# Norm and gate sums later, other PSUM banks, a chunk of products ahead of waits, and a compressed softmax spread over four slots: a three-layer transformer kernel on one core

## The chip, the cores and the metric

The kernel runs on one core of one Trainium2 chip. Its time is the device time of one execution in microseconds (us); lower is better. Engines are named as in the profile: PE is TensorE's matmul, PEld its weight load, DVE is VectorE, ACT is ScalarE, POOL is GpSimd, SP is SyncE (it issues most DMAs). PSUM is the memory into which PE writes.

## The reference, cut to what matters

512 positions, width 1024, float32. Three layers follow one another: a "forgetting" attention, a dilated attention, each with a gated addition behind it, and a block with a convolution branch, a sparse-attention branch with three parts (compressed, selected, window) and a feed-forward network.

```python
h = h + fox_mixer(rms_norm(h, fox_norm), fox_w_in, fox_b_f, fox_w_out)     # 16 heads of 64
h = h + (p[0] @ ple_w_up[0]) * sigmoid(h @ ple_w_gate[0])
h = h + dilated_mixer(rms_norm(h, dil_norm), dil_w_in, dil_w_out)          # 8 heads of 128, 3 patterns
h = h + (p[1] @ ple_w_up[1]) * sigmoid(h @ ple_w_gate[1])
x = rms_norm(h, final_norm)

def fox_mixer(h, w_in, b_f, w_out):
    q, k, v, z, f_logit = split(h @ w_in)
    c = cumsum(log_sigmoid(f_logit + b_f))                 # one gate per head and position
    s = q @ k.T / 8 + c[:, None] - c[None, :]              # causal
    return (softmax(s) @ v * silu(z)) @ w_out

def dilated_mixer(h, w_in, w_out):
    # q, k, v for 3 patterns (window 128 stride 1, 512 stride 4, 2048 stride 16), z once;
    # each pattern's softmax is weighted by its share of the common denominator
    return (o * silu(z)) @ w_out

def second_block(x, ...):
    hn = rmsnorm(x, norm1_g)
    a_b, a_c, a_x, q, kc, vc, ksl, vsl, kwn, vwn, g_nsa, g_merge = split(hn @ w_in)
    y_a = a_b * causal_dwconv(a_c * a_x, conv_a_w)
    q, k_sel, k_win = rope(rmsnorm(...))
    k_cmp, v_cmp = rmsnorm(compress(kc)), compress(vc)     # 31 compressed positions
    p_c = masked_softmax(q @ k_cmp.T / 8)                  # the compressed part
    y_b = g0 * p_c @ v_cmp + g1 * selected + g2 * window   # 8 heads of 64, 2 groups of keys
    x = x + (sigmoid(g_merge) gating of y_a @ w_a_out and y_b @ w_b_out) @ w_o
    hn = rmsnorm(x, norm2_g)
    g, u = split(hn @ w_ffn_in)
    return x + (silu(causal_dwconv(g) + b) * u) @ w_ffn_out
```

## The kernel before, in words

**Products.** Activations lie transposed, as eight tiles of 128 features by 512 positions. Each float32 operand is kept as two parts, a high half (`a0h`, `whi`) in the format that PE takes at full rate and the remainder (`a0l`, `wlo`), and `mm3` (L142) makes three products of each pair: high times high, high times low, low times high. These are the products of 128x512 on L144 to L146 (and L248 to L250 where positions are the rows).

**Weights.** `Weights` streams one 128x1024 unit at a time in a fixed plan: SP loads it (`wraw`), ACT copies the high half (`whi`, L74), DVE subtracts (`wlo`, L85). `pump` starts the next ones whenever a chunk of products is issued; the position of these instructions among the others of ACT, DVE and SP is therefore set by the order in which chunks are called. Every engine takes its own instructions in the order in which the program issues them.

**Chunks.** `t_unit` gives the products of one unit as two chunks of 12, and its evacuation behind the second. `k_outer` gives nine: `ko[0]` to `ko[7]` each make the nine products of one input tile with three units at once, into three accumulators, and `ko[8]` evacuates them. `n_chunk` gives eight chunks (two per unit) into four accumulators, with one evacuation after another in the last two. `narrow` gives two (placing the low halves, and 16 products). `run` calls a list, `weave` spreads attention slots evenly among chunks.

**PSUM.** `bank(tag)` hands out eight banks in turn: three `acc`, two `s`, two `t`, one `o`. Who asks for a bank waits until its former contents have been read.

**Norms.** A row's sum of squares is gathered by ACT (squares, L290) and POOL (`nacc`, L291), eight times. `norm_sums` (L295 to L303) then lets PE sum it over the partitions by products with one column; `norm_factors` makes the reciprocal root by a chain of small DVE operations (L310, L267 to L270); `norm_rows` spreads it over all partitions by PE and ACT (`rb`). Since products are made with unnormed data, `rb` is wanted only at the evacuation. In the fox mixer these are `fin1` and `fin2`, among the chunks on L581; `gate_sums` there starts the gate's chain (DVE L519 to L525), whose result `c` goes to DRAM and comes back spread over all partitions as `cb` (`load_c`), for the first softmax.

**Slots.** An attention step j is a slot: finish a softmax that is open (reciprocal and scaling, L637 and L640 or L642), transpose the probabilities of step j - LAG by PE into a `t` bank, copied by ACT (`pt` L695, `dpt` L836), then make the scores of step j in an `s` bank, which DVE reads first (L624, or L824 and L825), and ACT's exponential (L628). Every sixth or fourth slot adds a product with the values (`pv_step`, bank `o`), gated by `zh` and fed to the output products as `a0h`, `a0l` and so on (`feed`, L327 and L328). In the dilated mixer head h's slots are woven among `dz` (its gate, evacuated as `zh` L611, ACT's tanh L615, `zs` L616), `dq` and `dk` of head h + 1; the last slots (eight in the fox mixer, six in the dilated) are woven among the first chunks of the output projection by `mixer_out` (L591), which then closes the pool, opens the next stage's (`ple_open`, eight loads of the residual `hA`) and runs the rest.

**Second block.** L1300 runs the query units `nq` (the bank list is `n_chunk`'s default, `acc`, `acc`, `acc`, `s`) with `fin1` after its fourth chunk; ahead of it the gated addition's last unit is read out of its `acc` by ACT (`th`, L750). L1313 runs the first chunks of the convolution branch (`conv`), with small steps among them: `tr_k` transposes the keys `kd` (ACT, L1049) into a `t` or an `s` bank and splits them (`k00h`, `k00l` L1070), `tr_q` the queries into a `t` bank, `cmp_k3` the compressed keys `kcn`, copied by ACT as `kc` (L1125). The slots after that (L1279) hold, beside selected and window attention, the compressed part: `c_scores` in slots 1 and 19, `c_soft` (the softmax on [128, 16 x 32], DVE and one exponential) in slots 3 and 21, and `ct_step(p)`, its transposes, with step 2, 14, 26 and 38 of the transposes. `conv[5:]` and the merge gates are woven among them; `ev_ab` (L1173) multiplies an accumulator with `rb` and the convolution and feeds it (`b1h`).

Of the kernel before, what the change touches and what calls it, by code (L numbers as in the profile page):

```python
# [16 lines left out]
P = 128  # L17
# [110 lines left out]
class Net:  # L128
# [308 lines left out]
    def fox(self):  # L437
# [143 lines left out]
        run(ko[:7] + [fin1, ko[7], ch[0], ff[0], fin2, ko[8], ch[1], ff[1]] + ch[2:4])  # L581
        run([gate_sums] + ch[4:6] + [lambda: load_c(0), lambda: load_c(1)] + ch[6:])
# [8 lines left out]
    def mixer_out(self, tag, pair, es, res_src, i, slots):  # L591

        ko = self.k_outer([tag] * 3, [lambda a, n=n: self.ev_res(a, n) for n in range(3)], pair)
        weave(ko[:5], slots)
        es.close()
        self.ple_open(res_src, i)
        run(ko[5:])
        for n in range(3, 8):
            run(self.t_unit(tag, pair, self.full(), lambda a, n=n: self.ev_res(a, n), tag_ps="s" if n == 3 else "acc"))
# [167 lines left out]
    def dil(self):  # L767
# [122 lines left out]
        for h in range(8):  # L890
            if h % 4 == 0:
                vs = []
                for g in range(3):
                    vs += self.n_chunk("dv", residues if g else blocks, B, ev_v(g))
                weave(vs[:5], todo)
                run(vs[5:])
                todo = slots(h)
            ch = T("dz", ev_z(h))
            if h < 7:
                for g in range(3):  # L900
                    ch += T("dq", ev_q(h + 1, g)) + T("dk", ev_k(h + 1, g))
            n = 4 if h < 7 else 2
            weave(ch, todo[:n])
            todo = todo[n:]
# [42 lines left out]
    def block2(self):  # L947
# [174 lines left out]
        def cmp_k3():  # L1122
            p = self.bank("t")
            nc.tensor.transpose(p[:, :64], kcn.rearrange("p a d -> p (a d)"), self.ident[:64, :64])
            nc.scalar.activation(kc, p[:, :64], AF.Copy)  # L1125
# [114 lines left out]
        def c_soft(g):  # L1240
            sp, x = self.bank("o"), pcs[g]
            for qb in range(4):
                nc.tensor.transpose(sp[:, qb * P : (qb + 1) * P], x[:, qb * P : (qb + 1) * P], self.ident)
            pcs[g] = x = x.rearrange("p (q h k) -> p q h k", q=4, h=4)
            st = aa.tile([P, 2, 4, 4], F32, name="cst", tag="cst", bufs=1)
            bc = lambda y: y[:, :, :, None].broadcast_to([P, 4, 4, 32])
            m = mcmp[:, :P].rearrange("p (q k) -> p q k", q=4)[:, :, None, :].broadcast_to([P, 4, 4, 32])
            v.tensor_tensor(x, sp.rearrange("p (q h k) -> p q h k", q=4, h=4), m, ALU.add)
            v.tensor_reduce(st[:, 0], x, mybir.AxisListType.X, ALU.min)
            v.tensor_tensor(x, x, bc(st[:, 0]), ALU.subtract)  # L1250
            nc.scalar.activation(x, x, AF.Exp, scale=-1.0)
            v.tensor_reduce(st[:, 0], x, mybir.AxisListType.X, ALU.add)
            v.reciprocal(st[:, 1], st[:, 0])
            v.tensor_tensor(st[:, 1], st[:, 1], gc[:, :, 4 * g : 4 * g + 4], ALU.mult)
            v.tensor_tensor(x, x, bc(st[:, 1]), ALU.mult)
# [23 lines left out]
        def slot(j):  # L1279
            self.soft_end()  # L1280
            u = j - LAG
            if 0 <= u < 48:
                self.t_step(aa, pts, probs, u)
                if u % 12 == 2:
                    ct_step(u // 12)
            if j < 48:
# [3 lines left out]
                if j in (3, 21):  # L1290
                    c_soft(j // 21)
# [7 lines left out]
        ch = self.n_chunk("nq", lhs, A, ev_nq)  # L1299
# [11 lines left out]
        for i in range(4):  # L1311
            conv += T("ac", ev_ac(i)) + T("ax", ev_ax(i)) + T("ab", ev_ab(i))
        run([conv[0], gate_sums, conv[1], L(tr_k, 0, 0), L(tr_k, 0, 1), L(rope_k, 1), conv[2], cmp_k3, L(tr_q, 3), conv[3],  # L1313
             L(tr_k, 1, 0), tr_g, conv[4], L(tr_k, 1, 1)])
# [263 lines left out]
```

## Time and profile before

| | before |
|---|---|
| median of 3 runs | 1738.43 us (1738.42 to 1739.5) |
| profiled execution | 1738.31 us |
| its span | 1736.5 us |
| PE busy | 1718.7 us, 99% of the span |
| DVE, ACT, POOL busy | 967.3, 672.8, 111.0 us |
| share of the chain of waits on PE | 92% |
| DMA share of 16 engines | 30.0% (172.36 MB) |

The span is the time between the first and the last instruction of the profiled execution, 1.8 us less than its device time. A row of a timeline gives the start, the length, the engine, the line, the operation and its tiles, and in brackets the idle time before it with what ended that. Records of pipelined products overlap: a 128x512 product is shown as 0.39 us long, while one starts every 0.23 us.

### The profile page before, as it was taken

The numbers are of one execution on the slowest core, as the hardware profiler recorded it, in microseconds if no ns is written. First come the engines' busy times: TensorE is split into PE (matmuls) and PEld (weight loads), VectorE is DVE, ScalarE is ACT, GpSimd is POOL, SyncE is SP. The second block draws the span as 40 slices with busy tenths as digits, with TensorE's granted clock in tenths as the row PEclk, the third lists the DMA queues.
The fourth block names the chain that finished last, engine by engine and source line by source line (L and its number), as shares of the span: only waits on it lengthen the run. The fifth ranks groups of instructions, "written<-read, shape, count | busy, mean of one in ns | idle before, by whom it ended". The sixth has DMA issues, their size and how long they took to land.

```text
span 1736.5 us, 21611 instructions
## 1 busy us (share of the span) xinstructions
PE 1718.7 (99%) x8512; PEld 1401.6 (81%) x8512; DVE 967.3 (56%) x1692; ACT 672.8 (39%) x1146; POOL 111.0 (6%) x88
## 2 busy tenths in 40 slices
PE   8999999999999999999999999999999999999999
PEld 6777777888978889978878786777788888888887
DVE  6477774543354543354555677776554675566332
ACT  5466663522222222222245444555522433333220
POOL 2000000100000000000000411000000222111000
PEclk9999999999999999999999999999999999999999
DMA  5422224323221223222233422112243533223431
GB/s 166 141 93 86 91 74 139 122 93 130 90 85 61 85 73 97 85 85 73 74 111 120 156 99 73 49 61 86 73 141 120 165 108 101 96 97 98 145 97 61
DMA packets 57350, 173.74 MB, mean 100 GB/s; under 512 B 7441, under 2 KB 7953, under 8 KB 57249
## 3 DMA queue, kind: packets, MB, share of 16 engines
q1 hardware_dynamic: 57248, 172.36, 30.0%
q8 instruction: 67, 1.10, 0.3%
q14 instruction: 35, 0.28, 0.1%
HBM read 161.82 MB, written 10.52 MB: 99 GB/s over the span
## 4 chain that ended last, share of the span: by engine, by line
PE 92%; DVE 4%; ACT 2%; POOL 1%; issue 0%; DMA 0%; SPq 0%; ACTq 0%; DVEq 0%
PE acc L144 21%; PE acc L146 20%; PE acc L145 20%; PE acc L248 3%; PE acc L250 3%; PE acc L249 3%; PE o L700 2%; PE t L692 2%; PE s L144 1%; PE s L145 1%; PE s L146 1%; DVE wlo L85 1%; PE s L248 1%; PE s L679 1%; PE s L250 1%; PE s L249 1%
## 5 line engine op out<-in xcount | busy, mean ns | idle before, releaser
L85 DVE TENSOR_TENSOR wlo<-wraw,whi 128x1024 fp32r<-128x1024 f32 x267 | 347.8, 1309 | 137.9 <-ACT whi L74 137.8
L74 ACT ACTIVATE whi<-wraw 128x1024 fp32r<-128x1024 f32 x267 | 279.2, 1050 | 158.7 <-PE acc L145 68.2
L628 ACT ACTIVATE pr<-pr,st 128x512 f32<-128x512 f32 (+3 forms) x160 | 93.6, 586 | 155.3 <-DVE st L825 83.3
L291 POOL TENSOR_TENSOR nacc<-nacc,sq 128x512 f32<-128x512 f32 x35 | 47.9, 1376 | 1186.9 <-ACT sq L290 1186.4
L781 DVE TENSOR_TENSOR dqk<-acc,nacc 128x512 f32<-128x512 f32 x24 | 26.1, 1099 | 61.6 <-PE s L814 57.5
L695 ACT ACTIVATE pt<-t 128x512 f32<-128x512 f32 (+3 forms) x128 | 51.0, 424 | 19.7 <-PE t L692 19.3
L1413 ACT ACTIVATE fy<-fcv,fcw 128x512 f32<-128x512 f32 x22 | 18.0, 816 | 100.0 <-DVE fcv L1408 100.0
L1426 POOL TENSOR_TENSOR act<-fs,fu 128x512 f32<-128x512 f32 x22 | 43.3, 1969 | 191.0 <-DVE fu L1425 174.0
L692 PE MATMUL t<-ident,pr 128*128 128x128 f32 x320 | 51.1, 274 | 2.3 <-ACT pt L695 1.2
L692 PEld LDWEIGHTS t<-ident,pr 128*128 128x128 f32 x320 | 39.9, 140 | 14.5 <-DVE pr L640 1.6
L144 PE MATMUL acc<-a0h,whi 128*128 128x512 f32 x112 | 47.9, 427 | 1.2 <-DVE zh L611 1.2
L824 DVE SCALAR_TENSOR_TENSOR pr<-dist,s 128x128 f32<-128x128 f32 (+1 forms) x96 | 24.9, 315 | 42.2 <-PE s L818 42.2
L637 DVE RECIPROCAL st<-st 128x1 f32<-128x1 f32 x160 | 24.1, 158 | 40.4 <-ACT pr L628 40.4
L144 PE MATMUL acc<-b4h,whi 128*128 128x512 f32 x113 | 45.7, 404 | 0.0
L144 PE MATMUL acc<-b7h,whi 128*128 128x512 f32 x113 | 44.6, 395 | 0.0
L146 PE MATMUL acc<-b7h,wlo 128*128 128x512 f32 x113 | 44.6, 395 | 0.0
L145 PE MATMUL acc<-b7l,whi 128*128 128x512 f32 x113 | 44.4, 393 | 0.0
L146 PE MATMUL acc<-a0h,wlo 128*128 128x512 f32 x112 | 44.3, 395 | 0.0
L144 PE MATMUL acc<-b5h,whi 128*128 128x512 f32 x113 | 44.2, 391 | 0.0
L145 PE MATMUL acc<-a0l,whi 128*128 128x512 f32 x112 | 44.1, 394 | 0.0
L145 PE MATMUL acc<-a1l,whi 128*128 128x512 f32 x112 | 43.9, 392 | 0.2 <-DVE a1l L331 0.2
L145 PE MATMUL acc<-b4l,whi 128*128 128x512 f32 x113 | 44.1, 390 | 0.0
(1107 smaller groups left out, 4686.5 us busy)
## 6 DMA issues: line engine op xcount, KB each, us to landing
wraw<-in_dil_q SPq DMA_DIRECT2D x24, 512.0 KB, 3.3
wraw<-in_dil_k SPq DMA_DIRECT2D x24, 512.0 KB, 3.3
wraw<-in_dil_v SPq DMA_DIRECT2D x24, 512.0 KB, 3.3
wraw<-in_f_g SPq DMA_DIRECT2D x22, 512.0 KB, 3.5
wraw<-in_f_u SPq DMA_DIRECT2D x22, 512.0 KB, 3.5
wraw<-in_f_o SPq DMA_DIRECT2D x22, 512.0 KB, 3.4
wraw<-in_gate SPq DMA_DIRECT2D x16, 512.0 KB, 3.3
wraw<-in_b_gm SPq DMA_DIRECT2D x16, 512.0 KB, 3.5
```

What stands on the lines that cost most here:

```text
L74: nc.scalar.activation(hi, t, AF.Copy)
L85: self.nc.vector.tensor_tensor(lo, t, hi.bitcast(F32), ALU.subtract)
L144: mm(acc, wh, xh, start=start, stop=False)
L145: mm(acc, wh, xl, start=False, stop=False)
L146: mm(acc, wl, xh, start=False, stop=stop)
L248: self.nc.tensor.matmul(a, sh, mh, start=(k == 0), stop=False)
L249: self.nc.tensor.matmul(a, sh, ml, start=False, stop=False)
L250: self.nc.tensor.matmul(a, sl, mh, start=False, stop=(k == KT - 1))
L291: nc.gpsimd.tensor_tensor(self.nacc[i], self.nacc[i], sq, ALU.add)
L628: self.nc.scalar.activation(pr, pr, AF.Exp, scale=-1.0, bias=st[:, 0:1], accum_out=st[:, 1:2])
L692: nc.tensor.transpose(tp[:, c : c + P], pr[:, c0 + kb * P : c0 + (kb + 1) * P], self.ident)
L695: nc.scalar.activation(pts[h][:, self.KOFF[kb] : self.KOFF[kb] + b - a], tp[:, a:b], AF.Copy)
```

## The change

Six places are rewritten. In the fox mixer `fin1`, `fin2` and `gate_sums` are called later among the chunks. In `mixer_out`, used by both mixers, six chunks are woven among the last slots, and one fewer is left for after the pool is closed. In the dilated mixer's last head both chunks of `dz` are called ahead of its two slots, not one ahead of each. The `nq` chunk takes its accumulators in the order `s`, `t`, `acc`, `acc`. In the second block `conv[2]` is called ahead of `tr_k`, the later chunks move up, and `cmp_k3` takes an `s` bank. `c_soft` is cut into four steps, in four slots from 3 and 21 on, and the first `ct_step` goes with step 5 of the transposes. No computation is added or left out.

```diff
@@ -578,8 +578,8 @@
         lhs = lambda x, b: x[:, b * P : (b + 1) * P]
         ch = self.n_chunk("v", lhs, A, ev_v(0), ("s", "s", "t", "t"))
         ff = self.narrow("f", A, ev_f, "acc")
-        run(ko[:7] + [fin1, ko[7], ch[0], ff[0], fin2, ko[8], ch[1], ff[1]] + ch[2:4])
-        run([gate_sums] + ch[4:6] + [lambda: load_c(0), lambda: load_c(1)] + ch[6:])
+        run(ko[:8] + [ch[0], fin1, ch[1], ff[0], ch[2], fin2, ko[8], ch[3], ff[1], ch[4], ch[5]])
+        run([gate_sums] + [lambda: load_c(0), lambda: load_c(1)] + ch[6:])
         slots = [lambda j=j: slot(j) for j in range(48 + LAG + 2)]
         weave(self.n_chunk("v", lhs, A, ev_v(1), ("acc", "acc", "acc", "o")), slots[:3])
         weave(T("q", ev_q(1)) + T("k", ev_k(1)), slots[3:6])
@@ -591,10 +591,10 @@
     def mixer_out(self, tag, pair, es, res_src, i, slots):
 
         ko = self.k_outer([tag] * 3, [lambda a, n=n: self.ev_res(a, n) for n in range(3)], pair)
-        weave(ko[:5], slots)
+        weave(ko[:6], slots)
         es.close()
         self.ple_open(res_src, i)
-        run(ko[5:])
+        run(ko[6:])
         for n in range(3, 8):
             run(self.t_unit(tag, pair, self.full(), lambda a, n=n: self.ev_res(a, n), tag_ps="s" if n == 3 else "acc"))
 
@@ -900,7 +900,9 @@
                 for g in range(3):
                     ch += T("dq", ev_q(h + 1, g)) + T("dk", ev_k(h + 1, g))
             n = 4 if h < 7 else 2
-            weave(ch, todo[:n])
+            if h == 7:
+                run(ch)
+            weave(ch if h < 7 else [], todo[:n])
             todo = todo[n:]
         self.fox_like = False
         self.mixer_out("do", A, es, self.h_dram, 1, todo)
@@ -1120,7 +1122,7 @@
                 v.scalar_tensor_tensor(kcn[:, d, :], kcn[:, 0, :], ms[:64, 0, 48:49], self.ng[:64, 192:256], ALU.mult, ALU.mult)
 
         def cmp_k3():
-            p = self.bank("t")
+            p = self.bank("s")
             nc.tensor.transpose(p[:, :64], kcn.rearrange("p a d -> p (a d)"), self.ident[:64, :64])
             nc.scalar.activation(kc, p[:, :64], AF.Copy)
 
@@ -1237,22 +1239,31 @@
             pcs[g] = self.small.tile([P, S], F32, name="nacc", tag="nacc0", bufs=1)
             nc.scalar.activation(pcs[g], sp, AF.Copy)
 
-        def c_soft(g):
-            sp, x = self.bank("o"), pcs[g]
-            for qb in range(4):
-                nc.tensor.transpose(sp[:, qb * P : (qb + 1) * P], x[:, qb * P : (qb + 1) * P], self.ident)
-            pcs[g] = x = x.rearrange("p (q h k) -> p q h k", q=4, h=4)
-            st = aa.tile([P, 2, 4, 4], F32, name="cst", tag="cst", bufs=1)
+        cst = {}
+
+        def c_soft(g, step):
+
             bc = lambda y: y[:, :, :, None].broadcast_to([P, 4, 4, 32])
-            m = mcmp[:, :P].rearrange("p (q k) -> p q k", q=4)[:, :, None, :].broadcast_to([P, 4, 4, 32])
-            v.tensor_tensor(x, sp.rearrange("p (q h k) -> p q h k", q=4, h=4), m, ALU.add)
-            v.tensor_reduce(st[:, 0], x, mybir.AxisListType.X, ALU.min)
-            v.tensor_tensor(x, x, bc(st[:, 0]), ALU.subtract)
-            nc.scalar.activation(x, x, AF.Exp, scale=-1.0)
-            v.tensor_reduce(st[:, 0], x, mybir.AxisListType.X, ALU.add)
-            v.reciprocal(st[:, 1], st[:, 0])
-            v.tensor_tensor(st[:, 1], st[:, 1], gc[:, :, 4 * g : 4 * g + 4], ALU.mult)
-            v.tensor_tensor(x, x, bc(st[:, 1]), ALU.mult)
+            if step == 0:
+                sp, x = self.bank("o"), pcs[g]
+                for qb in range(4):
+                    nc.tensor.transpose(sp[:, qb * P : (qb + 1) * P], x[:, qb * P : (qb + 1) * P], self.ident)
+                pcs[g] = x = x.rearrange("p (q h k) -> p q h k", q=4, h=4)
+                cst[g] = aa.tile([P, 2, 4, 4], F32, name="cst", tag="cst", bufs=1)
+                m = mcmp[:, :P].rearrange("p (q k) -> p q k", q=4)[:, :, None, :].broadcast_to([P, 4, 4, 32])
+                v.tensor_tensor(x, sp.rearrange("p (q h k) -> p q h k", q=4, h=4), m, ALU.add)
+                return
+            x, st = pcs[g], cst[g]
+            if step == 1:
+                v.tensor_reduce(st[:, 0], x, mybir.AxisListType.X, ALU.min)
+                v.tensor_tensor(x, x, bc(st[:, 0]), ALU.subtract)
+                nc.scalar.activation(x, x, AF.Exp, scale=-1.0)
+            elif step == 2:
+                v.tensor_reduce(st[:, 0], x, mybir.AxisListType.X, ALU.add)
+                v.reciprocal(st[:, 1], st[:, 0])
+                v.tensor_tensor(st[:, 1], st[:, 1], gc[:, :, 4 * g : 4 * g + 4], ALU.mult)
+            else:
+                v.tensor_tensor(x, x, bc(st[:, 1]), ALU.mult)
 
         def ct_step(p):
             tp = self.bank("o")[:64]
@@ -1281,14 +1292,15 @@
             u = j - LAG
             if 0 <= u < 48:
                 self.t_step(aa, pts, probs, u)
-                if u % 12 == 2:
+                if u in (5, 14, 26, 38):
                     ct_step(u // 12)
             if j < 48:
                 s_step(j)
                 if j in (1, 19):
                     c_scores(j // 19)
-                if j in (3, 21):
-                    c_soft(j // 21)
+                for g in range(2):
+                    if 0 <= j - 3 - 18 * g < 4:
+                        c_soft(g, j - 3 - 18 * g)
             u -= 7
             if u >= 0 and u % 6 == 0 and u // 6 < 8:
                 pv_step(u // 6)
@@ -1296,7 +1308,7 @@
         lhs = lambda x, b: x[:, b * P : (b + 1) * P]
         T = lambda tag, ev, **k: self.t_unit(tag, A, self.full(), ev)
         gn = self.narrow("gn", A, ev_gn, "acc")
-        ch = self.n_chunk("nq", lhs, A, ev_nq)
+        ch = self.n_chunk("nq", lhs, A, ev_nq, ("s", "t", "acc", "acc"))
         run([ch[0], lambda: rope.extend(self.trig_tables(tmp))] + ch[1:4] + [fin1] + ch[4:])
         L = lambda f, *a: lambda: f(*a)
         kc_, vc_, kv = T("kc", ev_cmp(0)), T("vc", ev_cmp(1)), self.n_chunk("nkv", lhs, A, ev_nkv)
@@ -1310,8 +1322,8 @@
         conv = []
         for i in range(4):
             conv += T("ac", ev_ac(i)) + T("ax", ev_ax(i)) + T("ab", ev_ab(i))
-        run([conv[0], gate_sums, conv[1], L(tr_k, 0, 0), L(tr_k, 0, 1), L(rope_k, 1), conv[2], cmp_k3, L(tr_q, 3), conv[3],
-             L(tr_k, 1, 0), tr_g, conv[4], L(tr_k, 1, 1)])
+        run([conv[0], gate_sums, conv[1], conv[2], L(tr_k, 0, 0), L(tr_k, 0, 1), L(rope_k, 1), conv[3], cmp_k3, L(tr_q, 3), conv[4],
+             L(tr_k, 1, 0), tr_g, L(tr_k, 1, 1)])
         es2.close()
         self.open_b()
         es3 = ExitStack()
```

The order of instructions shows three of the places. First DVE at the fox start, where the small chain of the norm ends (L267 to L270) and the low half of the gate's weight is placed (L212), a piece of the difference:

```order
 L269 SCALAR_TENSOR_TENSOR rr<-rr 128x4
 L270 SCALAR_TENSOR_TENSOR rr<-rr 128x4
+L85 TENSOR_TENSOR wlo<-wraw,whi 128x1024
 L212 COPY whi<-wlo 128x8x32
+L85 TENSOR_TENSOR wlo<-wraw,whi 128x1024
 L572 CAST identb<-ident 128x128
 L573 TENSOR_REDUCE sel<-ident 128x32
```

Two weight subtractions that stood after the gate's chain now stand right behind the norm's chain.

Second DVE in the dilated mixer's last head. L824 and L825 read the scores of a slot, L637 and L640 finish its softmax, L611 and L616 evacuate `dz`. Before:

```order
L825 TENSOR_REDUCE st<-pr 128x1
L637 RECIPROCAL st<-st 128x1
L640 TENSOR_SCALAR pr<-pr,st 128x512
L824 SCALAR_TENSOR_TENSOR pr<-dist,s 128x128 x3
L825 TENSOR_REDUCE st<-pr 128x1
L85 TENSOR_TENSOR wlo<-wraw,whi 128x1024
L637 RECIPROCAL st<-st 128x1
L640 TENSOR_SCALAR pr<-pr,st 128x384
L611 SCALAR_TENSOR_TENSOR zh<-acc,rb 128x512
L616 SCALAR_TENSOR_TENSOR zs<-zs,zh 128x512
```

and in the changed kernel:

```order
L825 TENSOR_REDUCE st<-pr 128x1
L85 TENSOR_TENSOR wlo<-wraw,whi 128x1024
L637 RECIPROCAL st<-st 128x1
L640 TENSOR_SCALAR pr<-pr,st 128x512
L611 SCALAR_TENSOR_TENSOR zh<-acc,rb 128x512
L616 SCALAR_TENSOR_TENSOR zs<-zs,zh 128x512
L824 SCALAR_TENSOR_TENSOR pr<-dist,s 128x128 x3
L825 TENSOR_REDUCE st<-pr 128x1
L637 RECIPROCAL st<-st 128x1
L640 TENSOR_SCALAR pr<-pr,st 128x384
```

The evacuation moved ahead of one slot's softmax (L824 to L640 of the 128x384 row); the weight subtraction moved ahead of the finish of the slot before.

Third PE in the second block, at the first transposes of keys (L1067 before, L1069 after, as lines shifted by two). Rows between the first and the last product of a chunk are left out. Before:

```order
L146 MATMUL acc<-a7h,wlo 128x512
L1067 MATMUL t<-ident,kd 128x128 x4
L1067 MATMUL s<-ident,kd 128x128 x4
L144 MATMUL acc<-a0h,whi 128x512
...
L146 MATMUL acc<-a3h,wlo 128x512
L1124 MATMUL t<-ident,kcn 128x64
L1057 MATMUL t<-ident,qn 128x128 x4
L144 MATMUL acc<-a4h,whi 128x512
```

and in the changed kernel:

```order
L146 MATMUL acc<-a3h,wlo 128x512
L1069 MATMUL t<-ident,kd 128x128 x4
L1069 MATMUL s<-ident,kd 128x128 x4
L144 MATMUL acc<-a4h,whi 128x512
...
L146 MATMUL acc<-a7h,wlo 128x512
L1126 MATMUL s<-ident,kcn 128x64
L1059 MATMUL t<-ident,qn 128x128 x4
L144 MATMUL acc<-a0h,whi 128x512
```

Each group of transposes moved behind one more chunk of 12 products, and the transpose of `kcn` changed its bank from `t` to `s`.

## The prediction

> **What bounds the kernel now.** I read the page first: busy shares, then the chain of waits.
>
> ```profile
> span 1736.5 us, 21611 instructions
> ...
> PE 1718.7 (99%) x8512; PEld 1401.6 (81%) x8512; DVE 967.3 (56%) x1692; ACT 672.8 (39%) x1146; POOL 111.0 (6%) x88
> ...
> PE 92%; DVE 4%; ACT 2%; POOL 1%; issue 0%; DMA 0%; SPq 0%; ACTq 0%; DVEq 0%
> ```
>
> TensorE (PE) is the bound: it is busy for 1718.7 of 1736.5 us, and the chain runs over it for 92%. No product is taken away, so all there is to win is the time in which PE stood. The view of waits, taken for PE alone, puts that time down to causes:
>
> ```profile
> PE o L303 <- POOL nacc L291: 2.0, 1, 2.0
> PE acc L248 <- ACT th L750: 1.9, 1, 1.9
> PE t L1057 <- DVE k00l L1070: 1.6, 1, 1.6
> PE acc L144 <- DVE zh L611: 1.2, 1, 1.2
> PE t L692 <- ACT pt L695: 1.2, 1, 1.2
> PE s L678 <- DVE st L624: 1.1, 2, 0.7
> PE t L692 <- DVE pr L640: 0.8, 1, 0.8
> PE t L1067 <- ACT kd L1049: 0.6, 1, 0.6
> PE t L1067 <- ACT kc L1125: 0.4, 1, 0.4
> ```
>
> The columns are waiter, releaser, us in total, times, longest. These nine rows sum to 10.8 us, so a change of this kind can move about 0.6% and no more. Each row is answered by a piece of the diff, and the question for each piece is what is late next.
>
> One more thing moves PE's time: for two stretches of 3.4 us it ran at half clock. The timeline cut into windows shows the second:
>
> ```profile
> 1103.10:1106.50 3.40, 1.81 (x12) 1.35 (x12) 1.83 (x4) 2.22 (x6) 0.00 (x0) 1.00 0.35 141
> 1106.50:1109.90 3.40, 3.40 (x10) 2.66 (x9) 2.54 (x11) 2.92 (x8) 0.00 (x0) 0.51 0.00 0
> ```
>
> The columns are window, its length, busy us of PE, PEld, DVE, ACT and POOL, then the granted clock. PE was busy 1.81 us of the stretch before it and was then granted 0.51 for the next. A half-clock stretch costs half of 3.4, about 1.6 us after its edges. [...]
>
> **The change part by part.** All times below are on the clock of the trace before; a minus is a gain.
>
> *Fox start (fin1, fin2 and gate_sums later).*
>
> ```profile
> 24.96 1.05 PE L303 MATMUL o<-ones,nacc 128*128 128x1 f32 x8 [2.03 <-POOL nacc L291]
> ...
> 22.56 3.42 DVE L85 TENSOR_TENSOR wlo<-wraw,whi 128x1024 fp32r<-128x1024 f32 x2 [1.09 <-ACT whi L74]
> 26.05 0.16 DVE L310 TENSOR_SCALAR rr<-o 128x4 f32<-128x4 f32 x1
> ...
> 28.02 0.16 DVE L270 SCALAR_TENSOR_TENSOR rr<-rr 128x4 f32<-128x4 f32 x1
> ```
>
> PE waits for the last square sum on GpSimd. With ko[7] and ch[0] (about 2.1 and 2.7 us of products) ahead of the sums they come at 27.6, well after GpSimd ended at 24.9, so 2.0 goes, 2.1 with the gap's edges. What is late next: the chain of small DVE operations, 26.05 to 28.1, now starts at 28.6 and ends at 30.7, and the subtraction that makes the low half of the next v weight stands behind it on DVE (1.2 us, by the wlo rows), ready at 31.9. PE wants it for ch[2] at 31.5, as ch[2] comes sooner than before: about 0.4 of new waiting. The broadcast, its copy and the three evacuations are covered by ch[2]. The gate's chain ends some 4 us later, about 55 instead of 51.2; its row must pass through DRAM behind two more weight loads of SP's queue, and I put its arrival at 62.4 against the first use near 62.6. If it is late, two free s banks give some 8 us before PE notices. Term **−1.7**; bounds −2.1 (chain no issue) and −0.8 (the weight 1.3 late).
>
> *mixer_out: six chunks of ko woven, not five.* It concerns both mixers. The fox waits around 253 (0.8, L640) stay: the slot concerned still follows ko[0]. One more chunk comes between slots, one more change between large and small products, about 0.2 (two edges of 0.1: a 0.50 record where 0.39 is usual). In the dilated mixer ko[6] alone now stands between the last attention product and ko[7].
>
> ```profile
> 892.37 1.07 DVE L854 TENSOR_TENSOR zh<-o,zs 128x512 f32<-128x512 f32 x1 [6.99 <-PE o L850]
> 894.14 0.69 DVE L328 TENSOR_TENSOR a7l<-zh,a7h 128x512 fp32r<-128x512 f32 x1 [0.70 <-ACT a7h L327]
> ...
> 893.48 0.63 ACT L327 ACTIVATE a7h<-zh 128x512 fp32r<-128x512 f32 x1 [3.90 <-DVE zh L854]
> ```
>
> a7l is ready 2.75 us after PE has left the attention product at 892.1, and a chunk of ko is nine products, about 2.2 us, so ko[7] waits 0.4. The residual loads are asked for a chunk later; their first use follows ko[7], a chunk and the 2.75 us on. Term **+0.5**; bounds 0 and +1.0.
>
> *Head 7: both dz chunks ahead of its two slots.*
>
> ```profile
> 871.86 0.50 PE L144 MATMUL acc<-a0h,whi 128*128 128x512 f32 x1 [1.25 <-DVE zh L611]
> ...
> 865.27 0.81 DVE L824 SCALAR_TENSOR_TENSOR pr<-dist,s 128x256 f32<-128x256 f32 x3
> 869.46 1.22 DVE L85 TENSOR_TENSOR wlo<-wraw,whi 128x1024 fp32r<-128x1024 f32 x1
> 871.12 0.68 DVE L611 SCALAR_TENSOR_TENSOR zh<-acc,rb 128x512 f32<-128x512 f32 x1
> ...
> 867.55 1.04 ACT L74 ACTIVATE whi<-wraw 128x1024 fp32r<-128x1024 f32 x1
> ...
> 876.34 0.57 ACT L836 ACTIVATE dpt<-t 128x512 f32<-128x512 f32 x1
> ```
>
> ko[0] wants a third acc bank, held until DVE reads dz out of it (zh). DVE is about a slot behind PE: at 865.27 it works on scores that PE had finished at 860.4. In the new order zh stands ahead of the next slot's softmax but behind the slot in work and a wlo, which cannot start before whi ends on ACT at 868.6: wlo to 869.8, reciprocal and scaling to 870.4, zh to 871.0 instead of 871.8. So about 0.8 is won here, and 0.9 of the wait stays. But now the tanh of dz and zs (0.6 and 0.7) go ahead of the next slot's softmax on both engines. Slot A's probabilities reach the exponential at 873.5 instead of 869.6; the t copies and the two later softmaxes follow, and the copy of 876.34 comes at about 878.1, ending 878.7. PE, which would start the attention product at 876.2, reads that copy in its third block, at 877.0: it waits 1.6, less what it was ahead. Term **+1.4**, by this ledger; bounds −1.2 (the whole wait goes and the softmax catches up in the 3.7 us of a slot) and +2.2 (t and s banks cost 0.4 each on top). I take the ledger, since both queues' order is fixed and every duration has a row.
>
> *nq chunk in banks s, t, acc, acc.*
>
> ```profile
> 985.16 0.50 PE L248 MATMUL acc<-whi,a0h 128*128 128x512 f32 x1 [1.93 <-ACT th L750]
> ...
> 984.54 0.57 ACT L750 ACTIVATE th<-acc 128x512 f32<-128x512 f32 x1
> ...
> 989.46 2.60 POOL L291 TENSOR_TENSOR nacc<-nacc,sq 128x512 f32<-128x512 f32 x2 [3.77 <-ACT sq L290]
> ```
>
> The last gate's acc is read at 985.1, behind a weight on ACT. With s and t first, PE starts 12 products (2.7 us) elsewhere, and needs an acc only after the read. The norm sums come 2.1 earlier, 991.4, and GpSimd ends at 992.06: the first eight sums need the first accumulator, done at 990.8, the others want the second at 992.3. It just fits. Term **−2.1**; bounds −2.1 and −1.3 (GpSimd late by 0.8).
>
> *Conv order and cmp_k3 in bank s.*
>
> ```profile
> 1064.38 0.66 PE L1057 MATMUL t<-ident,qn 128*128 128x128 f32 x4 [1.63 <-DVE k00l L1070]
> ...
> 1063.64 0.68 DVE L1070 TENSOR_TENSOR k00l<-t,k00h 128x512 fp32r<-128x512 f32 x1
> ...
> 1066.45 0.63 ACT L1049 ACTIVATE kd<-kd 128x512 f32<-128x512 f32 x1 [3.95 <-DVE kd L1048]
> ```
>
> conv[2] (12 products, 2.7 us) runs while ACT copies kd, so the 0.6 goes. cmp_k3 no longer takes a t bank, so the transposes of q need not wait for k00l: they have a chunk more in front of them too, and the 1.6 goes. The next transposes wait for kc no longer (0.4): that was the same t bank. They need kd of 1066.45, done at 1067.1, and come at 1067.7, so that cover is thin; if it fails it costs up to 0.6. One change of kinds less, since tr_k(1, 1) joins tr_g: 0.2. With the edges of 0.15 at each wait, tr_k(1, 1) ends 3.4 earlier. Term **−3.4**; bounds −3.5 and −2.2.
>
> *Compressed softmax over four slots, first ct_step three slots later.*
>
> ```profile
> 1092.39 0.68 DVE L1248 TENSOR_TENSOR nacc<-o,mcmp 128x512 f32<-128x512 f32 x1
> ...
> 1095.30 0.69 DVE L1252 TENSOR_REDUCE cst<-nacc 128x16 f32<-128x512 f32 x1 [0.78 <-ACT nacc L1251]
> ...
> 1104.93 0.68 DVE L624 CUSTOM_DVE_ANT_0 pr<-s,mwin 128x512 f32<-128x512 f32 x1
> ...
> 1104.20 0.37 ACT L695 ACTIVATE pt<-t 128x256 f32<-128x256 f32 x1
> ...
> 1104.62 0.66 PE L692 MATMUL t<-ident,pr 128*128 128x128 f32 x4 [1.19 <-ACT pt L695]
> ```
>
> DVE ran the whole softmax at 1092.39 to 1097.1, 4.0 us of work and a 0.78 wait for ACT, and each later slot's softmax came late. PE then stood at 1097, 1098.6, 1102.4, 1104.6 and 1105.7: 0.4, 0.8, 0.3, 1.35 and 0.65 with edges, 3.5 in all. The work stays 4.0; spread out, the 0.78 goes and three steps of it pass before DVE is wanted again. The first three waits should go. The last two hang on the convolution's read and its feed (b1h, then the copy of 1104.20), behind them the softmax of 1104.93: they come some 2 us earlier, and PE also. Of the 2.0 I leave about all in place. Term **−1.6**; bounds −3.5 (all five go) and 0.
>
> **The sum.** −1.7 + 0.5 + 1.4 − 2.1 − 3.4 − 1.6 = −6.9. The half clock before 1110 follows on the stalls that shrink, and I count half of its 1.6 as gone without −0.8 being certain: between −6.9 and −8.5, I take −7.4. The profiled execution took 1738.3 (1.8 beside its span) and the median is 1738.43, so nothing is corrected: **1731**, or −0.4%.
>
> **The rivals.**
> 1. *Every wait goes and nothing is late next.* For it: each piece puts 2 to 3 us of products ahead of a wait of 2 us or less. Against it: DVE is a slot behind at head 7 whichever order it has. The lower bounds of the terms give −2.1 + 0 − 1.2 − 2.1 − 3.5 − 3.5 = −12.4, and a half-clock stretch less: 1724 to 1726.
> 2. *The waits move.* DVE's and ACT's work is the same, so in the stages where they and not the order bind, PE's earlier arrival is waited off a few slots on: head 7 costs its 2.2, the compressed softmax gives 0, the fox start 0.8. With the convolutions' lower −2.2 and −1.3 for the banks: −0.8 + 1.0 + 2.2 − 1.3 − 2.2 = −1.1, so 1735.5 to 1739 with the clock's ±1.6. For it: all of PE's neighbours there work in order. Against it: at 1064 and 985 a bank and not an engine's work was missing.
> 3. *Slower: head 7's lateness is paid in every slot.* Six slots follow it, one chunk of ko each. If the copy of slot n always ends after PE wants the t bank again, ACT's work in a slot stands bare: exponential 0.9, whi 1.0, copy 0.6, 2.5 in all, six times 15 in place of the 1.4. The total is then +6.2, near 1745. It decides once ACT and DVE need more for a slot than PE's 3.7 (t and s 1.5, chunk 2.2); ACT's 2.5 and DVE's 3.4 by the same rows say no, by little for DVE.
>
> **How the numbers follow.** Forecast (gain of 4 to 10 us) 0.64; rival 1 0.13; rival 2 0.18; rival 3 0.05. A measurement of this kernel can tell about 0.2%, 3.5 us, from no change: faster means under 1734.9, slower over 1741.9. The forecast's upper end and rival 1 give 0.77 faster; rival 2 and an odd end of 3 give 0.18 the same; 0.05 slower. The range reaches from rival 1's upper edge to the middle of rival 2: **1726 to 1736.5**.
>
> **What would show it.** In the changed kernel's waits for PE, the rows of L303, th, k00l, kd and kc should be gone; the fox start should show a wait of under 1 us for a wlo; the third acc of ko[0] should still wait for zh, about 1 us, and the attention product after it for a dpt copy, 1 to 2 us; ko[7] of the dilated mixer for a7l; one t and one s wait should remain in the compressed stage. PE's last product of that stage should come 5 to 7 us earlier. I am wrong if head 7 shows no new wait, if the first stage's gain is eaten before the mixer ends, or if half-clock stretches number none or more than three.

## The result, and the profile after

The changed kernel took 1730.09 us (median of 4 runs, 1729.0 the fastest), the kernel before 1738.43. The two medians give a ratio of 0.9952; the ratio on record is 0.9944, interval 0.9931 to 0.9957. One execution here took 1892.05 us at a granted clock of 0.851 and one of a kernel below took 4543.93; the medians count them, the ratios do not. The forecast was 1731. The page of the changed kernel's profiled execution (1729.0 us) answers to the first rows shown of before:

```profile
span 1727.2 us, 21619 instructions
...
PE 1714.4 (99%) x8512; PEld 1398.8 (81%) x8512; DVE 966.0 (56%) x1692; ACT 672.2 (39%) x1146; POOL 111.0 (6%) x88
...
PE 96%; DVE 2%; ACT 1%; DMA 0%; issue 0%; SPq 0%; ACTq 0%; DVEq 0%
```

As many products as before, and the chain of waits goes over PE for 96% instead of 92%. The other engines' share of the chain halved or better. The waits of PE (waiter, releaser, us in total, times, longest):

```profile
PE o L449 <- ACT cb L446: 2.3, 1, 2.3
PE acc L144 <- ACT whi L62: 1.4, 1, 1.4
PE o L844 <- ACT dpt L836: 1.2, 1, 1.2
PE t L692 <- ACT pt L695: 1.1, 1, 1.1
PE t L692 <- DVE pr L640: 0.8, 1, 0.8
PE acc L144 <- DVE zh L611: 0.6, 1, 0.6
PE s L678 <- DVE st L624: 0.4, 1, 0.4
PE s L249 <- DVE wlo L85: 0.3, 1, 0.3
PE s L814 <- DVE pr L824: 0.3, 1, 0.3
...
PE acc L145 <- DVE a7l L328: 0.2, 1, 0.2
PE t L835 <- ACT dpt L836: 0.2, 1, 0.2
```

Gone are the rows of nacc (2.0), th (1.9), k00l (1.6), kd (0.6) and kc (0.4). New are dpt at L844, a wlo, pr L824, a7l and dpt at L835, each at a place that the prediction names or next to it; zh shrank from 1.2 to 0.6. The first two rows belong to no edit. The first stands ahead of the kernel's first products and is 2.3 in the kernel before too, as the longest row of its view, which the prediction's list leaves out. The second is a wait for the first weights: it was 1.1 and 0.4 in two other executions below, and the kernel before has none.

Since both kernels make the same 8512 products, the start of one and the same product can be compared in both profiles. How far the changed kernel is ahead (minus) after each place, and what that place brought, in us:

```
place                             drift after it   this place   forecast
start of the kernel                    +0.45          +0.45         -
fox start                              -1.28          -1.73        -1.7
fox mixer_out                          -1.16          +0.1         +0.2
half-clock stretch at 376              -2.75          -1.6          0
head 7 of the dilated mixer            -1.11          +1.6         +1.4
dilated mixer_out                      -0.56          +0.55        +0.3
nq banks                               -2.69          -2.1         -2.1
conv order, cmp_k3                     -5.92          -3.2         -3.4
compressed softmax, with the stretch   -9.30          -3.4         -1.6 and about -0.5
```

A half-clock stretch is 3.4 us in which PE ran at half clock (granted clock 0.50 from 376.09 to 379.50 in the profile of before). The prediction has one forecast for mixer_out in both mixers, 0.5; it is split here into its 0.2 for one more change of kinds, in the fox mixer, and the rest in the dilated one.

### The profile page after: what moved, and what is told of

The parts are those of the page before. It is cut to its first block, busy times and chain, and to the rows that moved or that the text cites. A ratio compares the mean times of both kernels' runs of the same rounds, so it can differ in the third digit from the quotient of the medians.

```text
span 1727.2 us, 21619 instructions
## 1 busy us (share of the span) xinstructions
PE 1714.4 (99%) x8512; PEld 1398.8 (81%) x8512; DVE 966.0 (56%) x1692; ACT 672.2 (39%) x1146; POOL 111.0 (6%) x88
## 4 chain that ended last, share of the span: by engine, by line
PE 96%; DVE 2%; ACT 1%; DMA 0%; issue 0%; SPq 0%; ACTq 0%; DVEq 0%
PE acc L144 22%; PE acc L145 21%; PE acc L146 21%; PE acc L248 3%; PE acc L250 3%; PE acc L249 3%; PE o L700 2%; PE t L692 2%; PE s L144 1%; PE s L145 1%; PE s L146 1%; PE s L249 1%; PE s L248 1%; PE s L679 1%; PE s L250 1%; PE s L678 1%
## 5 line engine op out<-in xcount | busy, mean ns | idle before, releaser
L824 DVE SCALAR_TENSOR_TENSOR pr<-dist,s 128x128 f32<-128x128 f32 (+1 forms) x96 | 24.9, 314 | 42.2 <-PE s L818 42.2
L637 DVE RECIPROCAL st<-st 128x1 f32<-128x1 f32 x160 | 23.8, 158 | 38.6 <-ACT pr L628 38.6
L144 PE MATMUL acc<-b6h,whi 128*128 128x512 f32 x113 | 44.1, 390 | 0.0
L146 PE MATMUL acc<-b6h,wlo 128*128 128x512 f32 x113 | 44.0, 390 | 0.0
L146 PE MATMUL acc<-b4h,wlo 128*128 128x512 f32 x113 | 44.0, 389 | 0.0
(1108 smaller groups left out, 4680.7 us busy)
```

Source lines behind the costliest of these rows:

```text
L144: mm(acc, wh, xh, start=start, stop=False)
L146: mm(acc, wl, xh, start=False, stop=stop)
```

## The experiments

The theory to be tested is the prediction's ledger, its list of what each engine has to do in which order and for how long: each place has its own price, the prices add, and the two places that lost (head 7, mixer_out) lost by what their queues hold. The rival behind most runs is that waits only move, so that undoing a piece changes nothing. The later fox start and the convolution's chunk in front were not run alone; for these two the starts of the products have to do.

**The change again.** The kernel as changed.

> The changed kernel itself, once more, so that the others of this group have it on the same chip. If half-clock stretches of TensorE (about 1.6 us each) are a matter of the execution and not of the program, the times of this kernel and of the kernel before each spread in steps of about 1.6 us, and the profile may show one, two or none; if they are tied to the stalls that the change removed, the changed kernel shows none in this profile either. Either way 1729 to 1731.

Five runs gave 1728.44, 1730.23, 1730.43, 1730.45 and 1731.87; the kernel before ran nine times beside it, from 1736.99 over 1738.43 to 1738.56 and 1740.16 to 1740.76. Both spread in steps of 1.4 to 1.8, and the mean granted clock of an execution goes with them: 1.000 at 1728.44, 0.999 at 1730.2 to 1730.5, 0.998 at 1731.87. Half clock for 3.4 of 1728 us lowers that mean by 0.001, so it counts the stretches: none, one, two (and one to three in the kernel before, 0.999 to 0.997). With equal numbers the two kernels lie 6.6 apart: 1736.99 and 1730.4 with one, 1738.5 and 1731.87 with two. This execution's profile (1730.23) has one half-clock stretch, at 375, that the profile of the 1729.0 run has not. The windows around it, columns as in the prediction; first the 1729.0 run of the changed kernel:

```profile
370.21:373.62 3.41, 3.41 (x21) 3.17 (x19) 0.00 (x0) 0.00 (x0) 0.00 (x0) 1.00 0.00 0
373.62:377.03 3.41, 3.41 (x16) 2.91 (x16) 1.84 (x11) 1.06 (x1) 0.00 (x0) 1.00 0.00 0
```

then this run of the same kernel:

```profile
370.30:373.72 3.42, 3.42 (x21) 3.22 (x19) 0.00 (x0) 0.00 (x0) 0.00 (x0) 1.00 0.00 0
373.72:377.13 3.41, 3.41 (x10) 2.80 (x10) 1.83 (x11) 1.06 (x1) 0.00 (x0) 0.50 0.00 0
```

The same instructions, once at clock 1.00 and once at 0.50. Whether a stretch comes is a matter of the execution. In the profiles read here they stand at two places of the program: behind the dilated mixer's norm sums (L303, 16 one-column products; from 376.09 in the kernel before, from 373.72 here) and behind the stalls of the second block's slots (from 1106.54 in the kernel before).

PE's records leave no gap at the norm sums. In the 3.4 us ahead of the stretch PE started 3 products of 128x512 in the kernel before (372.67 to 376.09) and 4 in this execution (370.30 to 373.72), where 3.4 us full of them, one every 0.23 us, make about 15. But in the 1729.0 run PE started only 3 from 371.52 to 374.93 as well, and the clock stayed at 1.00 in these 3.4 us and in the next. So how few large products there are does not decide alone; what does is not shown.

So medians of kernels that differ by 1 us say less than profiles, and times are compared below with equal numbers of stretches.

**Head 7 undone.**

```diff
-            if h == 7:
-                run(ch)
-            weave(ch if h < 7 else [], todo[:n])
+            weave(ch, todo[:n])
```

> The changed kernel with the dz chunks of head 7 woven with the two slots as before. Theory (the ledger of both queues): running both chunks first costs 1.4 to 1.5 us, so this is faster than the changed kernel by 1.4 to 1.5, about 1728.5; TensorE waits 1.25 for zh at ko[0] and no longer 1.2 for the copy dpt. Rival (the waits only move, the loss at head 7 is made up later in the mixer): no difference, 1730.

1728.61 (1728.53 to 1728.7), 1.8 under the median of the changed kernel beside it. All five executions hold one stretch (0.999), as do the changed kernel's at 1730.2 to 1730.5, so like is compared with like: 1.6 to 1.8. Its waits show the old stall and no dpt:

```profile
PE acc L144 <- DVE zh L611: 1.2, 1, 1.2
PE t L692 <- ACT pt L695: 1.1, 1, 1.1
```

By the starts of the products head 7 is at no loss or gain against before (0.0), where the changed kernel loses 1.6. The loss is not made up later: the rival falls.

**mixer_out undone.**

```diff
-        weave(ko[:6], slots)
+        weave(ko[:5], slots)
...
-        run(ko[6:])
+        run(ko[5:])
```

> The changed kernel with five chunks of the output projection woven among the last slots in both mixers, not six. Theory: the sixth chunk cost 0.5 to 0.8 (0.2 in each mixer for one more change between large and small products, 0.3 in the dilated mixer for a7l), so this is faster by 0.5 to 0.8, about 1729.4, and the wait for a7l is gone. Rival (the sixth chunk covers waits for the slots, which come back): slower by 0.3 to 1.

1731.42 by the median, 1.0 above the changed kernel's, which alone would read as a loss. But four of the five executions, the profiled one among them, hold two stretches (0.998), and the changed kernel with two took 1731.87; with none it is 1728.15 against 1728.44. So it is 0.3 to 0.45 faster by the times, of which the pair without a stretch is one execution each. The products' starts say 0.65: no loss in the dilated mixer (-0.03) nor in the fox mixer (0.0), where the changed kernel loses 0.55 and 0.1. The wait for a7l is gone. By the starts the theory holds (0.5 to 0.8); by the times the gain falls short of its lower end. The rival, a loss, falls.

**dz evacuated first.** Both chunks stay ahead of the slots, but zh is issued right behind its products, and the rest of the gate's silu (ACT's tanh and the product `zs`) goes after the two slots.

```diff
+                    if last:                      # in t_unit, second chunk of head 7's dz; its pump is left out
+                        run([evac(st["acc"])])
...
+                if h == 7:                        # in ev_z
+                    late.append(rest)
+                    return None
...
+                run(ch + [todo[0], self.w.pump, todo[1]])
+                run(late)
```

> The changed kernel; in head 7 the dz evacuation (zh) is issued right behind its products, ahead of the weight subtraction and of the open softmax, and the tanh and the product behind it go after the two slots. Theory (what costs at head 7 is what stands ahead of zh and of the two softmaxes in DVE's and ACT's queues): the waits for zh (0.6), dpt (0.2 and 1.2) and pr (0.3) all go, 2.2 to 2.3 us faster than the changed kernel, about 1727.8. Rival (DVE and ACT are a slot behind there by their amount of work, whatever the order): the dpt wait stays at about 1, gain 0 to 1.

1726.84, 3.6 under the changed kernel's median; 1725.2 against 1728.4 for the fastest of each. All four waits went, and by the starts of the products the place wins 1.6 where the changed kernel loses 1.6. In the changed kernel DVE and ACT had been doing this:

```profile
863.35 0.69 DVE L825 TENSOR_REDUCE st<-pr 128x1 f32<-128x512 f32 x1
865.87 1.23 DVE L85 TENSOR_TENSOR wlo<-wraw,whi 128x1024 fp32r<-128x1024 f32 x1 [1.83 <-ACT whi L74]
...
867.60 0.68 DVE L611 SCALAR_TENSOR_TENSOR zh<-acc,rb 128x512 f32<-128x512 f32 x1
868.99 0.69 DVE L616 SCALAR_TENSOR_TENSOR zs<-zs,zh 128x512 f32<-128x512 f32 x1 [0.70 <-ACT zs L615]
...
870.89 0.61 ACT L628 ACTIVATE pr<-pr,st 128x384 f32<-128x384 f32 x1 [1.45 <-DVE st L825]
```

and in this kernel:

```profile
865.36 0.69 DVE L832 TENSOR_REDUCE st<-pr 128x1 f32<-128x512 f32 x1
865.96 0.68 DVE L615 SCALAR_TENSOR_TENSOR zh<-acc,rb 128x512 f32<-128x512 f32 x1
866.92 0.16 DVE L641 RECIPROCAL st<-st 128x1 f32<-128x1 f32 x1 [0.28 <-ACT pr L632]
...
868.82 0.62 ACT L632 ACTIVATE pr<-pr,st 128x384 f32<-128x384 f32 x1 [0.50 <-DVE st L832]
```

In the changed kernel DVE stood 1.83 for a weight's high half and 0.70 for the tanh, with the evacuation that PE wanted queued behind the first and a softmax behind the second. From the reduction to the exponential of the next slot it took 7.5 us there and 3.5 here. DVE was late by its order, not by its load: the rival falls. Expected were 2.2 to 2.3, the sum of the four waits; it was 3.2 by the starts and by the fastest times 3.3. The view of waits counts idle time only from the end that it shows for the product before, and each of the four stalls is 0.1 to 0.3 longer from start to start. The run moves the weight subtraction and the tanh at once, so how the loss divides between them is not shown.

**Banks alone.** The kernel before, with the nq bank list and cmp_k3's bank changed and nothing else.

> The kernel before with the two changes of banks alone (nq chunk in s, t, acc, acc; cmp_k3 in s), and the order of the convolution chunks as before. Theory (what was missing at both places was a bank): the wait for th (1.9) goes, 2.1 us by the products' starts, and of the waits at tr_q and tr_k those for k00l (1.6) and kc (0.4) go while that for kd (0.6) stays: 4.2 to 4.5 us faster up to the slots, about 1734. Rival (the bank only uncovers the next wait, and the chunk in front does the work): the kd and k00l waits are replaced by waits for the s bank or a copy, and less than 1 us is won at the conv stage: about 1736.

One run, with two stretches as most of before's: 1735.08. The nq place wins 2.1, as in the changed kernel. At the conv stage the bank wins 1.6 at tr_q, and 0.6 of it goes again at the next transposes, 1.0 in all. The places in the timeline of PE:

```profile
1060.21 0.66 PE L1057 MATMUL t<-ident,qn 128*128 128x128 f32 x4
1064.69 0.66 PE L1067 MATMUL t<-ident,kd 128*128 128x128 f32 x4 [1.08 <-ACT kd L1049]
```

The wait for k00l is gone from the first; the second now waits 1.08 for kd, which had been covered by that stall. So of the 3.2 of the whole edit at this place the banks alone bring 1.0, and the other 2.2 need the chunk in front: the bank uncovers the next wait, and the chunk covers it. Up to the slots 3.1 were won, where I had expected 4.2 to 4.5. At nq the theory holds, at the conv stage more of the rival than I had allowed.

**Compressed softmax in one slot.** All four steps in slots 3 and 21 again; the first ct_step stays with step 5.

> The changed kernel with all four steps of the compressed softmax in one slot again (3 and 21), the first ct_step still with step 5. Theory (spreading is what helped, by letting slot softmaxes pass on DVE): the waits for st (0.7 at the s bank) and pr come back, 1.0 to 1.5 us slower than the changed kernel by the products' starts in that stage. Rival (it is enough that ct_step comes three slots later): no difference in that stage.

1732.28, one run with one stretch, 1.8 to 2.1 over the changed kernel with one (the kernel before took 1738.59 beside this run and 1738.56 beside the changed kernel). The wait for the s bank is back, and larger:

```profile
PE s L678 <- DVE st L624: 2.0, 2, 1.6
```

By the products' starts it is 2.2 slower in that stage, more than the 1.0 to 1.5 expected, so the later ct_step on its own is worth nothing: the stage is 0.4 behind the kernel before. Spreading is what won.

**Softmax steps later still.** Steps 1 to 3 in slots 7 to 9, the first ct_step with step 6.

> The changed kernel with steps 1 to 3 of the first compressed softmax moved to slots 7, 8 and 9, behind the convolution's evacuation at slot 6, and the first ct_step with step 6. Theory (the waits left at slot 8, pt 1.15 and st 0.41, come from DVE reaching the convolution's product late because two steps of the compressed softmax stand ahead of it): both go, 1.5 to 1.8 us faster in that stage, and the half-clock stretch that followed them in some executions goes too. Rival (DVE is late there by the work of the convolution itself and the weight subtraction): the pt wait stays at 0.7 or more.

1733.52, slower than the changed kernel by 1.7 where the numbers of stretches are equal (1733.6 against 1731.9, 1731.9 against 1730.3). The pt wait did go, as the theory had it, and 1.5 us were won at slot 8. Then:

```profile
1104.91 0.55 PE L692 MATMUL t<-ident,pr 128*128 128x128 f32 x3 [0.82 <-DVE pr L642]
1107.49 0.63 PE L1271 MATMUL o<-ident,nacc 128*64 128x128 f32 x4 [2.03 <-DVE nacc L1266]
```

the steps themselves came too late for ct_step, and a slot's softmax stood behind them; 3.3 were lost, and in the profiled execution a stretch of half clock followed at 1108 (records of 128x512 products 0.63 us long instead of 0.39). Here the waits moved and grew.

**Norm sums in two groups.** The dilated mixer's eight one-column sums as four and four, with ko[7] between them.

```diff
-        run(ko[:7] + [fin1, ko[7], dk[0], fin2, ko[8], dk[1]])
+        run(ko[:7] + [fin1a, ko[7], fin1, dk[0], fin2, ko[8], dk[1]])
```

> The changed kernel with the eight one-column sums of the dilated mixer's norm in two groups of four, with the nine products of ko[7] between them. Theory (a half-clock stretch follows when one window of 3.4 us holds too little work of the array, and the 2.8 us of one-column products are such a window): the stretch at 375 never comes, the slower of the times of the changed kernel (1.6 us steps) become rarer, median about 1729, at 0.2 us more for one more change of kinds. [...]

1728.58. Three executions took 1728.48 to 1728.58 and hold no stretch, one took 1730.23 and holds one. Of the changed kernel's eight executions, taken in two lots, two held none. The profile shows clock 1.00 in the place of the stretch, and one more change of kinds cost nothing that the starts show. The two kernels below have the sums in two groups as well: seven of their nine hold no stretch. Together that is 10 of 13 against 2 of 8. The place of a stretch is known for the profiled executions alone, and the three with the sums in two groups have none at all (granted clock 1.000). So stretches became rarer and the median came out near 1729, as the theory had it. That too little work in 3.4 us is the cause is not shown by this: the 1729.0 run has the sums in one group, and the clock stayed at 1.00 there.

**The pieces together.** Head 7 with zh first, mixer_out undone, sums in two groups, and at the fox start one line ahead of the norm's chain, `self.w.finish()`, so that the weight subtraction which ch[2] wants does not stand behind the chain.

> The changed kernel with what the runs so far point to: the early dz evacuation (3.1 us by its profile), five chunks in mixer_out (0.5), the two groups of norm sums (no half-clock stretch at 375), and at the fox start the weight subtraction that ch[2] wants issued ahead of the norm's chain (the 0.44 wait for wlo). Theory (the stages are far apart and their terms add): 1728.5 without a half-clock stretch, less 3.1 + 0.5 + 0.4: 1724.4, or 1726 in the executions with the stretch near 1095; median 1724.4 to 1726. Rival (what is won early is lost in later stages, or the subtraction delays the norm's chain): 1726.5 or more.

1724.55 (1723.29 to 1725.91), 0.9919 of before, interval 0.9905 to 0.9932. The fox start now wins 2.3 instead of 1.7, head 7 wins 1.6, the dilated mixer_out loses nothing. The executions without a stretch took 1723.29 to 1724.55 against the 1724.4 expected, those with one 1725.9 against 1726: the terms add.

> The same, and the first compressed softmax in slots 3, 4, 6 and 7 (only steps 2 and 3 go behind the convolution's evacuation), its first ct_step with step 6. Theory (the waits at slot 8 come from DVE's work ahead of the convolution's product, 1.1 us of it step 2): the pt wait of 1.15 shrinks to 0.2 or less and none for nacc takes its place, 1.0 to 1.3 faster than the one without: 1723.2 to 1724.8. Rival (as with slots 7 to 9, the wait moves to the ct_step's transposes or to a slot softmax behind): no gain, or slower.

1723.49 (1723.44 to 1723.63), 0.9910 of before, interval 0.9896 to 0.9923. What PE still waits for, start included:

```profile
PE o L453 <- ACT cb L450: 2.3, 1, 2.3
PE t L698 <- DVE pr L646: 0.8, 1, 0.8
PE t L698 <- ACT pt L701: 0.7, 1, 0.7
PE acc L144 <- ACT whi L62: 0.5, 1, 0.5
PE s L684 <- DVE st L630: 0.4, 1, 0.4
...
```

The pt wait went from 1.15 to 0.7, half of what was expected, and no wait for nacc came: neither the theory nor the rival. By the starts it gains 0.5 at slot 8 over the run above, whose fastest execution took 1723.29, since its first weights came 0.9 sooner there; the times alone do not tell the two apart. Both beat the kernel before and the changed one.

## Why the prediction was right

**Bound and size.** PE's own waits were what could be won, and 1731 met 1730.09. That it came within 1 us is in part luck, since the median can fall on any of the steps of the changed kernel's times (1728.4, 1730.3, 1731.9). Without half-clock stretches the places sum to -6.6 by the drift of the products (-1.73 + 0.1 + 1.6 + 0.55 - 2.1 - 3.2 - 1.8; the last is from the run with head 7 undone, which has a stretch where before has one, at a clock of 0.52 from 1096.10 to 1099.50), where I had -6.9. The rest, about 1.7 of the measured 8.3, is one stretch fewer in the middle execution: two in before, one in the changed kernel. Two sums of the prediction do not come out of their parts: half of 1.6 added to -6.9 gives -7.7 and not -7.4, and the middle of the second rival lies at 1737.3 and not at 1736.5, where the range ends.

**Fox start, -1.7 against -1.73.** The chain on DVE came late as worked out, and the wlo row is there:

```profile
27.98 0.95 PE L303 MATMUL o<-ones,nacc 128*128 128x1 f32 x8
...
32.31 0.50 PE L249 MATMUL s<-wlo,a2h 128*128 128x512 f32 x1 [0.28 <-DVE wlo L85]
```

The sums wait for nothing, and 0.28 of idle time is 0.44 from start to start. No wait for the gate's row shows.

**mixer_out, +0.5 against +0.66.** The a7l wait is there (0.23); the fox mixer cost 0.1 and not 0.2. The parts that the prediction names, 0.2 for each mixer and 0.4 for a7l, make 0.8, so its 0.5 was no sum of them.

**Head 7, +1.4 against +1.6.** This was the term against the grain of the edit, and it came as the ledger of the two queues had it: third acc still waiting for zh, and behind it the attention product:

```profile
868.34 0.50 PE L144 MATMUL acc<-a0h,whi 128*128 128x512 f32 x1 [0.56 <-DVE zh L611]
...
876.03 0.92 PE L844 MATMUL o<-dpt,v 128*128 128x256 f32 x4 [1.24 <-ACT dpt L836]
```

The copy dpt that PE waited for started at 875.40, which with the drift of 2.74 is 878.14 on the clock of before; the prediction had 878.1. What it had wrong is PE's own arrival: it took PE to be ahead by the earlier zh, but the waits for the t and s banks, 0.2 and 0.3 of idle time, used that up, and PE began the attention product 0.1 later than before. Of the zh wait 0.56 stayed; the 0.9 in the prediction does not follow from its own 1.25 less 0.8. That the softmax would catch up within a slot, my lower bound, did not happen.

**nq banks, -2.1 against -2.1.** GpSimd ended in time; no row for nacc is left.

**Conv order, -3.4 against -3.2.** The cover for the second kd held in the changed kernel. The run with banks alone shows what comes without the chunk: a wait of 1.08.

**Compressed softmax, -1.6 against -1.8.** The first three waits went and the two at slot 8 stayed: pt 1.15 and st 0.41 are in the waits above, with the cause that I named, since taking DVE's work away ahead of the convolution shrank the pt wait.

**Half clock.** The step that was weak. I took the stretch to follow on the stalls and to go half the time when they shrink, and named it as a sign of being wrong if there were none. The changed kernel's first profile, the 1729.0 run, has none, the second has one: the sign came, and the step was wrong. Near slot 8 of the second block the 1729.0 run is as empty as the run with mixer_out undone, and full clock follows:

```profile
1094.40:1097.80 3.40, 1.84 (x14) 1.47 (x13) 2.67 (x6) 1.21 (x3) 0.00 (x0) 1.00 0.47 154
1097.80:1101.20 3.40, 3.40 (x21) 2.86 (x20) 2.26 (x10) 3.40 (x10) 0.00 (x0) 1.00 0.00 0
```

In the run with mixer_out undone half clock follows:

```profile
1095.24:1098.65 3.41, 1.86 (x14) 1.48 (x13) 2.68 (x6) 1.24 (x3) 0.00 (x0) 1.00 0.47 154
1098.65:1102.06 3.41, 3.41 (x10) 2.71 (x9) 2.28 (x11) 3.41 (x10) 0.00 (x0) 0.50 0.00 0
```

PE was busy for 1.84 us ahead of full clock and for 1.86 ahead of half clock (1.81 in the kernel before), and at 375 its records show no idle time, so what sets a stretch off stays open. A stretch cost 1.4 to 1.8 us by the steps in the times, where I had 1.6; that it could go either way by so much, as the second rival's range has it, was my estimate. The number I took, 0.5, was about 1.2 too small, and within the range.

**The rivals.** That every wait goes (1724 to 1726) failed at head 7 and slot 8; it is nearly what the repaired kernels reach. That the waits move was true in the changed kernel of head 7 and of a7l only; it shows again where less was changed (banks alone, 1.08 for kd) or more (softmax steps later still, 2.03 for nacc). Head 7 paying in every slot did not come: its loss stayed 1.6 from the attention product on.

## What to carry to other kernels

An order of chunks sets the order in three other queues: before moving an evacuation ahead, list what stands between it and the engine's present work, for here a weight subtraction that itself waited (1.83 us) and a tanh (0.70) together made a rearrangement lose 1.6 that could win 1.6. Where a wait is removed, look for the one that it covered (kd, 1.08), and split long side work so that no piece stands ahead of what PE wants, but not so late that its own reader waits (2.0). Under 2 us, compare the starts of the same products in two profiles; a median of five runs mixes in steps of 1.6 us that are none of the edit's.

## What the runs showed of the hardware that was not expected

Half-clock stretches of 3.4 us, about 1.6 us lost by each, came at two places of the program in some executions and not in others of the same kernel. At one place PE had no gap over 1.2 us in the kernel before; at the other its records show none at all, while it made one-column products for 2.8 us. They make the steps in the times: 1728.4, 1730.3 and 1731.9 for the changed kernel. How little PE did just ahead does not decide alone: at the slots 1.84 us busy of 3.40 were followed by a clock of 1.00 in one run and 1.86 of 3.41 by 0.50 in another; at the one-column products 3 starts of large products in 3.4 us were followed by 1.00 in one execution and 4 by 0.50 in another. What decides is not shown. With the one-column products in two groups, nine large ones between, all three profiled executions had a granted clock of 1.000, and 10 of 13 executions held no stretch against 2 of 8.
